# A two-layer encoder trunk on one core: the second mixer's constants get their own place and load one stage earlier, and GpSimd adds a norm's shift

## The chip, the cores and the metric

The kernel is one program on one core of a Trainium2 chip. The metric is the device time of one execution in microseconds (us); lower is better. The engines are named as in the profile: PE is TensorE (matmul), DVE is VectorE, ACT is ScalarE, POOL is GpSimd, and SP is the engine whose queue issues all the DMAs here. Each engine works through its own instructions in the order in which they stand.

## The reference, cut to what matters

The input is `x`, 256 tokens of 2048 channels in float32. Two layers follow one another; each has a mixer and a gated feed-forward, each closed by a residual sum and a layer norm with scale g and shift b:

```
for layer in range(2):
    if layer == 0: y = ab_mixer(x, ...)      # local attention and gated recurrence
    else:          y = cd_mixer(x, ...)      # pooling mixer and grouped-query attention
    x = layer_norm(DN_ALPHA * x + y, ln_mix_g[layer], ln_mix_b[layer])
    f = swiglu(x, w_gate, w_up, w_down)      # hidden width 5632
    x = layer_norm(DN_ALPHA * x + f, ln_ffn_g[layer], ln_ffn_b[layer])

def layer_norm(x, g, b):  return (x - mean) * rsqrt(var + eps) * g + b

def cd_mixer(x, ...):
    c_x, d_q, d_k, d_v = split(x @ w_in)     # 1024, 1024, 256, 256 columns
    y_c = multiscale_pool(c_x, ...)          # centred means over 2, 4, 8, 16 tokens, then a matmul
    q = rope(rms_norm(d_q, q_norm)); k = rope(rms_norm(d_k, k_norm))
    return concat(y_c, attention(q, k, d_v)) @ w_out
```

Here the place of interest is the seam between the two layers: the last norm of layer 0 (`ln_ffn_g[0]`, `ln_ffn_b[0]`) and the first projection of `cd_mixer`.

## The kernel before, in words

**Split matmuls.** Every float32 operand is split into a high part and a low part, and a product is three matmuls (`mm3`: low by high, high by high, high by low). A weight comes in halves of 128x1024 elements (512 KB). `load_half` issues the DMA into a tile `raw`, ACT casts it to `whi` (line 127), DVE subtracts to get `wlo` (line 128). There are four `raw` tiles, so a fifth load waits until the first half has been split. The `whi`/`wlo` pairs stand in a ring: four in the pool `wp`, and more in pools that a stage opens (`open_ring`); after `open_ring`, the first 12 halves still go to the four of `wp` alone. A cast waits until PE is done with the half that held its slot.

**Tokens.** The 256 tokens are two groups of 128 (`tok` 0 and 1). `mm_chunk` runs one output block of 512 columns for both groups: half by half for both groups, or, where `tok_major` is set, all halves for group 0 and then all for group 1. The outputs of a block are PSUM banks `acc`, of which there are three, so a third block's second bank is the one that the evacuation of an earlier block gives back.

**Down phase and norm.** The feed-forward has three phases, each ending in four output blocks `n` of the down projection. In the last phase `end` is true: at block `n == 1` `load_gb` loads the norm's `gam` and `bet` (1024 KB each, broadcast to all partitions), and the last block runs with `tok_major`. After each group's last matmul, `norm(tok)` takes mean and variance on DVE, the reciprocal root `rstd` on POOL (line 246, a power), centres on DVE (line 323), scales on ACT (line 337), and appends `flip(tok)` to a list. `flip` transposes the four 512-column pieces on PE (line 124, at places in the PE order that are pinned, inside the following tok_major pass), and ACT and DVE read the transposed pieces and add the shift from `betT`, which gives the next stage's operands `xTh` and `xTl`. The residual rows `res` themselves need the shift too: `flip` puts that addition into the list `idle_work`, from which a later `mm_chunk` takes two at a time and gives them to DVE, behind its weight splits (line 369).

**The mixer's constants.** `cd_mixer` opens its pool at the seam and allots the rotary tables `cc` and `sn`, the norm weights `nwq` and `nwk`, `pscale`, `rcount` and the pooling matrix `band` there. The first projection block (`kv`, tok_major) is followed by `constants_in`, which loads them; `band` passes through two of the four `raw` tiles (as `braw`) and is cast by ACT (line 875), and `nwq` is multiplied by a number on DVE (line 868). The function `kv` then evacuates the first block: ACT casts `dvh` from the bank, DVE subtracts `dvl`, ACT squares into `junk` (line 885), POOL takes `rstd`, and DVE writes `rx` from the bank (line 889), which is the last read of that bank.

**What sets the order.** The program is written through a layer whose scheduler orders each engine's instructions by priority and by its own model of time; `high_priority` raises a priority, `issue_after` and `keep_in_program_order` fix an order. Code that is moved therefore moves other instructions too.

Of the kernel before, what the change touches and what calls it, by code (L numbers as in the profile page):

```python
# [11 lines left out]
F32 = mybir.dt.float32  # L12
F32R = mybir.dt.float32r
# [5 lines left out]
P = 128  # L19
# [61 lines left out]
def trunk(ctx: ExitStack, tc: tile.TileContext, a, out):  # L81
# [216 lines left out]
    def new_stats():  # L298
        return [sm.tile([P, 4, 6], F32, tag=f"st{t}", name=f"st{t}", bufs=1) for t in range(NT)]

    def residual_tools(res, gam, bet, betT, stats):

        def evac(tok, n, psum, start, last):
            r = res[tok][:, n * NCH : (n + 1) * NCH]
            if start:
                nc.vector.scalar_tensor_tensor(r, r, ALPHA, psum, op0=mult, op1=add)
            else:
                nc.vector.tensor_tensor(r, r, psum, op=add)
            if last:
                nc.vector.bn_stats(stats[tok][:, n, :], r)  # L310

        def norm(tok, xT=None, out_rows=None):
            mv = sm.tile([P, 2], F32, tag="mv", name="mv", bufs=2)
            nc.vector.bn_aggr(mv, stats[tok])
            rstd = rstd_of(mv[:, 1:2], 1)

            def cols(j):
                s = slice(j * NCH, (j + 1) * NCH)
                return res[tok][:, s], gam[:, s], bet[:, s]

            def centre(j):
                r, g, _ = cols(j)
                return nc.vector.scalar_tensor_tensor(r, r, mv[:, 0:1], g, op0=sub, op1=mult)  # L323

            def scale(j):
                r, _, b = cols(j)
                return nc.vector.scalar_tensor_tensor(r, r, rstd[:, 0:1], b, op0=mult, op1=add)  # L327

            def store(j):
                nc.sync.dma_start(out_rows[tok * P : (tok + 1) * P, j * NCH : (j + 1) * NCH], cols(j)[0])  # L330

            if out_rows is None:
                for j in range(4):
                    dve = centre(j)
                for j in range(4):
                    r = cols(j)[0]
                    act = nc.scalar.activation(r, r, AF.Copy, scale=rstd[:, 0:1])
                ahead[:] = [dve.ins, act.ins]
                pending.append(flip(tok, xT))
            else:  # L340
                for j in (3, 0, 1):
                    tc.keep_in_program_order(centre(j))
                r, _, b = cols(3)
                nc.scalar.activation(r, r, AF.Copy, scale=rstd[:, 0:1])
                nc.gpsimd.tensor_tensor(r, r, b, op=add)
                for j in (0, 1, 2):
                    if j == 2:
                        tc.keep_in_program_order(centre(j))
                    tc.keep_in_program_order(scale(j))
                    store(j)  # L350
                store(3)

        def flip(tok, xT):
            for j in range(4):
                s = slice(j * NCH, (j + 1) * NCH)
                r = res[tok][:, s]
                with tc.high_priority(offset=1000):
                    t = mxp() if j % 2 else trp()
                    for k in range(4):
                        tc.keep_in_program_order(transpose(t[:, k * P : (k + 1) * P], r[:, k * P : (k + 1) * P], ident))  # L360
                    for part in range(2):
                        for k in range(4):
                            hi, lo = xT[0][tok][:, 4 * j + k, :], xT[1][tok][:, 4 * j + k, :]
                            tk, bk = t[:, k * P : (k + 1) * P], betT[:, 4 * j + k : 4 * j + k + 1]
                            if part == 0:
                                act = nc.scalar.activation(hi, tk, AF.Identity, bias=bk)
                            else:
                                dve = nc.vector.scalar_tensor_tensor(lo, tk, bk, hi.bitcast(F32), op0=add, op1=sub)
                idle_work.append(lambda r=r, s=s: nc.vector.tensor_tensor(r, r, bet[:, s], op=add))
                if j == 3:  # L370
                    ahead[:] = [dve.ins, act.ins]
                yield j

        return evac, norm
# [9 lines left out]


    def out_proj(w, order, groups, res, gb):
        evac, norm = residual_tools(res, *gb, new_stats())
        lhs = y_lhs(groups)
        xT = new_xT()
        for n in range(4):  # L390
            outs = [acc() for _ in range(NT)]
            halves = [(w[n, 2 * g + i], two(4 * g + 2 * i)) for g in order for i in range(2)]

            def after(tok):
                with tc.high_priority(offset=1000 if n == 3 else 0):
                    evac(tok, n, outs[tok], True, True)
                    if n == 3:
                        norm(tok, xT)

            mm_chunk(halves, lhs, outs, tok_major=(n == 3), after=after)  # L400
        return xT
# [96 lines left out]
    def ffn(layer, xT, res, mix_pool, close_mix, keep, last):  # L498
# [29 lines left out]
                if next(making[0], "end") is None:  # L528
                    later.append([3, make])

        nxt = None
        groups = {}
        for pi, chunks in enumerate(PHASES):
            end = pi == len(PHASES) - 1
# [15 lines left out]
            if end:  # L550
                stack.close()
                open_banks("uses")
                open_ring(keep(f"er{layer}"), 4)
                open_ring(later_pool(stack, f"e{layer}"), 3)
                fp = later_pool(stack, f"g{layer}")
                nxt = None if last else new_xT()
            stats = new_stats()
            evac, norm = residual_tools(res, None, None, None, stats)
            for n in range(4):
                if end and n == 1:  # L560
                    evac, norm = residual_tools(res, *load_gb(fp, layer, "ffn"), stats)
                outs = [acc() for _ in range(NT)]
                halves = [(a[f"down{layer}"][n, 2 * c + i], two(4 * ci + 2 * i)) for ci, c in enumerate(chunks) for i in range(2)]

                def after(tok):
                    with tc.high_priority(offset=1000 if end and n == 3 else 0):
                        evac(tok, n, outs[tok], pi == 0, end)
                        if end and n == 3:
                            norm(tok, nxt, out if last else None)

                mm_chunk(halves, y_lhs(gl), outs, tok_major=(end and n == 3), after=after)
# [280 lines left out]
            do[kind](i, outs)  # L852


    def cd_mixer(mp, xT, yT):
        cc = mp.tile([P, NT, P], F32, name="cc", bufs=1)
        sn = mp.tile([P, NT, P], F32, name="sn", bufs=1)
        nw = {n: mp.tile([P, P], F32, name=f"nw{n}", bufs=1) for n in ("q", "k")}
        pscale = mp.tile([P, 64], F32, name="pscale", bufs=1)[:, :8]
        rcount = mp.tile([P, 4, 2, EDGE], F32, name="rcount", bufs=1)  # L860
        band = mp.tile([P, 4, NT, T], F32R, name="band", bufs=1)

        def constants_in():
            nc.sync.dma_start(cc, a["rope_cos"])
            nc.sync.dma_start(sn, a["rope_sin"])
            for n in ("q", "k"):
                nc.sync.dma_start(nw[n], a[f"d_{n}_norm"][0:1, :].to_broadcast([P, P]))
            nc.vector.tensor_scalar(nw["q"], nw["q"], QSCALE, None, op0=mult)
            nc.sync.dma_start(pscale, a["pool_scale"])
            nc.sync.dma_start(rcount, a["rcount"])  # L870
            for g in range(0, 4, 2):
                s = slice(g, g + 2)
                raw = wp.tile([P, 2, NT, T], F32, tag="raw", name="braw", bufs=4)
                nc.sync.dma_start(raw, a["band"][:, s])
                nc.scalar.copy(band[:, s], raw)

        lhs = x_lhs(xT)
        st = {}

# [95 lines left out]
        for c, (kind, _) in enumerate(cd_plan()):  # L975
            outs = [acc() for _ in range(NT)]
            mm_chunk([(a["cd_in"][c, n], two(2 * n)) for n in range(8)], lhs, outs, tok_major=(c == 0))
            if c == 0:
                with tc.high_priority(offset=150):
                    constants_in()  # L980
            if kind == "kv":
                kv(outs)
            elif kind[0] == "q":
                q(kind[1], outs)
            else:
                pool(kind[1], outs)
# [23 lines left out]
    def layer_end(i, w, groups, yT, last):  # L1010
# [10 lines left out]
        xT = out_proj(w, groups, yT, res, load_gb(fp, i, "mix"))  # L1021
        return ffn(i, xT, res, fp, close, keep, last)

    xT = layer_end(0, a["ab_out"], AB_OUT_GROUPS, yT, False)
    yT = [new_yT() for _ in range(4)]
    with tc.tile_pool(name="cd", bufs=1, reuse_waits="tile") as mp:
        cd_mixer(mp, xT, yT)
    layer_end(1, a["cd_out"], CD_OUT_GROUPS, yT, True)
    kept.close()

# [113 lines left out]
```

## Time and profile before

| what | value |
|---|---|
| median of 3 runs | 2211.68 us (2210.59 to 2213.93) |
| profiled execution, its own time | 2208.31 us |
| its span, first to last instruction | 2206.5 us |
| mean granted TensorE clock | 0.997 of full speed |
| PE / DVE / ACT / POOL busy | 2176.5 / 1564.1 / 1053.2 / 42.2 us |
| DMA, mean | 191 GB/s, 57.0% of 16 engines |

The profiled execution lies 1.8 us above its span, and 3.4 us under the median. PE is busy nearly all the time, so a stall of PE is time of the whole; what other engines do counts where PE waits for it.

### The profile page before, as it was taken

The page shows a single profiled execution, that of the slowest core. Times are in us where ns is not written, and L with a number is a line of the kernel's source. Part 1 is how long each engine was busy: PE and PEld are TensorE (multiplying, and loading weights), DVE is VectorE, ACT ScalarE, POOL GpSimd, SP SyncE. Part 2 cuts the span into 40 slices and gives each one's busy share as a digit, 9 for nine tenths or more (in the row PEclk, how much of TensorE's full clock was granted, in tenths as well). Part 3 has the DMA queues.
Part 4 walks back from the last instruction along what each step waited for, and adds up shares of the span by engine and source line. Part 5 has one row for each costly group of instructions (what it writes and reads, how often), then busy time and mean ns, then how long its engine had stood idle before and what let it go on. Part 6 is the DMA issues. An engine that isn't in the chain of part 4 may idle for free. (4 is left out here: it accounts for less than half of the span.)

```text
span 2206.5 us, 26606 instructions
## 1 busy us (share of the span) xinstructions
PE 2176.5 (99%) x10048; PEld 1806.2 (82%) x10048; DVE 1564.1 (71%) x1960; ACT 1053.2 (48%) x1276; POOL 42.2 (2%) x43
## 2 busy tenths in 40 slices
PE   8999999999999999999999989999999999999997
PEld 7888888888888888888888778888888878888886
DVE  6886688567538787577877676677357886668865
ACT  6445544546435445445544554555344554445442
POOL 0000001000000000000000000000000000000001
PEclk9999999999999999999999999999999999999999
DMA  8555546684636565565557363657456555655573
GB/s 288 163 163 180 171 126 191 210 276 141 231 117 240 178 206 186 190 228 185 189 180 269 127 206 124 213 169 237 154 172 225 184 180 194 212 198 183 179 249 114
DMA packets 112562, 420.64 MB, mean 191 GB/s; under 512 B 13744, under 2 KB 16304, under 8 KB 105520
## 3 DMA queue, kind: packets, MB, share of 16 engines
q1 hardware_dynamic: 112432, 418.93, 57.0%
q8 instruction: 79, 1.29, 0.2%
q14 instruction: 51, 0.42, 0.1%
HBM read 416.78 MB, written 2.10 MB: 190 GB/s over the span
## 5 line engine op out<-in xcount | busy, mean ns | idle before, releaser
L128 DVE TENSOR_TENSOR wlo<-raw,whi 128x1024 fp32r<-128x1024 f32 (+1 forms) x673 | 818.8, 1224 | 435.2 <-ACT whi L127 425.0
L127 ACT CAST whi<-raw 128x1024 fp32r<-128x1024 f32 (+1 forms) x673 | 704.8, 1052 | 827.3 <-PE acc L290 329.0
L290 PE MATMUL acc<-whi,xTl 128*128 128x512 f32 x1056 | 418.3, 397 | 13.2 <-DVE rx L889 6.5
L290 PE MATMUL acc<-whi,xTh 128*128 128x512 f32 x1056 | 415.3, 393 | 0.0
L290 PE MATMUL acc<-wlo,xTh 128*128 128x512 f32 x1056 | 412.7, 393 | 1.0 <-DVE wlo L128 1.0
L290 PEld LDWEIGHTS acc<-whi,xTl 128*128 128x128 f32 x1056 | 199.8, 189 | 54.2 <-ACT whi L127 8.2
L290 PEld LDWEIGHTS acc<-wlo,xTh 128*128 128x128 f32 x1056 | 199.5, 189 | 42.6 <-DVE wlo L128 1.9
L290 PEld LDWEIGHTS acc<-whi,xTh 128*128 128x128 f32 x1056 | 199.8, 189 | 39.2
L290 PE MATMUL acc<-whi,yTl 128*128 128x512 f32 x512 | 200.4, 392 | 0.1
L290 PE MATMUL acc<-whi,yTh 128*128 128x512 f32 x512 | 199.5, 390 | 0.0
L290 PE MATMUL acc<-wlo,yTh 128*128 128x512 f32 x512 | 197.7, 390 | 0.0
L290 PE MATMUL aside<-whi,xTl 128*128 128x512 f32 x336 | 131.2, 390 | 0.4 <-ACT g L480 0.4
L290 PE MATMUL bside<-whi,xTl 128*128 128x512 f32 x336 | 131.2, 390 | 0.1
L290 PE MATMUL bside<-whi,xTh 128*128 128x512 f32 x336 | 131.0, 390 | 0.0
L290 PE MATMUL aside<-whi,xTh 128*128 128x512 f32 x336 | 131.0, 390 | 0.0
L290 PE MATMUL bside<-wlo,xTh 128*128 128x512 f32 x336 | 128.2, 390 | 0.0
L290 PE MATMUL aside<-wlo,xTh 128*128 128x512 f32 x336 | 128.1, 390 | 0.0
L290 PEld LDWEIGHTS acc<-wlo,yTh 128*128 128x128 f32 x512 | 96.1, 188 | 20.4 <-DVE wlo L128 0.5
L290 PEld LDWEIGHTS acc<-whi,yTl 128*128 128x128 f32 x512 | 96.1, 188 | 19.9 <-DVE yTl L973 0.3
L290 PEld LDWEIGHTS acc<-whi,yTh 128*128 128x128 f32 x512 | 96.2, 188 | 19.3
L128 DVE TENSOR_TENSOR sl<-z,sh 128x2048 fp32r<-128x2048 f32 x44 | 100.7, 2289 | 6.2 <-ACT sh L127 5.6
L439 ACT CAST sh<-rs 128x1536 fp32r<-128x1536 f32 x44 | 65.2, 1483 | 74.7 <-DMA rs<-in_gu 32.9
(257 smaller groups left out, 3109.5 us busy)
## 6 DMA issues: line engine op xcount, KB each, us to landing
raw<-in_gu SPq DMA_DIRECT2D x264, 512.0 KB, 4.7
raw<-in_down SPq DMA_DIRECT2D x176, 512.0 KB, 3.6
raw<-in_ab_in SPq DMA_DIRECT2D x127, 512.0 KB, 4.1
rs<-in_gu SPq DMA_DIRECT2D x44, 1024.0 KB, 5.8
raw<-in_cd_in SPq DMA_DIRECT2D x40, 512.0 KB, 4.1
raw<-in_ab_out SPq DMA_DIRECT2D x32, 512.0 KB, 4.4
raw<-in_cd_out SPq DMA_DIRECT2D x32, 512.0 KB, 4.4
x<-in_xT SPq DMA_DIRECT2D x8, 256.0 KB, 6.4
```

Of the source, the lines that this page charges most:

```text
L127: nc.scalar.copy(hi, src)
L128: return nc.vector.tensor_tensor(lo, src, hi.bitcast(F32), op=sub).ins
L290: ins = nc.tensor.matmul(o, lhs[a], rhs[b], start=start and n == 0, stop=stop and n == 2)
L439: nc.scalar.copy(hi[:, :3], raw[:, :3])
```

## The change

`cd_constants` is a new function with the body of `constants_in`; it is called in the last down phase of layer 0, at block `n == 1` and ahead of `load_gb`, and takes its tiles from a pool `cdc` that is opened ahead of the ring `er0` and kept open through the mixer. `residual_tools` gets an argument `defer`: `out_proj` passes True and so keeps the list `idle_work`; the feed-forward's norm (only layer 0's has a `flip`) now gives the eight additions of `bet` to POOL, right where `flip` is done with a piece.

```diff
-    def residual_tools(res, gam, bet, betT, stats):
+    def residual_tools(res, gam, bet, betT, stats, defer=False):
...
-                idle_work.append(lambda r=r, s=s: nc.vector.tensor_tensor(r, r, bet[:, s], op=add))
+                if defer:
+                    idle_work.append(lambda r=r, s=s: nc.vector.tensor_tensor(r, r, bet[:, s], op=add))
+                else:
+                    nc.gpsimd.tensor_tensor(r, r, bet[:, s], op=add)
...
     def out_proj(w, order, groups, res, gb):
-        evac, norm = residual_tools(res, *gb, new_stats())
+        evac, norm = residual_tools(res, *gb, new_stats(), True)
...
             if end:
                 stack.close()
                 open_banks("uses")
+                cdp = None if last else keep("cdc")
                 open_ring(keep(f"er{layer}"), 4)
...
             for n in range(4):
+                if cdp and n == 1:
+                    consts.extend(cd_constants(cdp))
                 if end and n == 1:
                     evac, norm = residual_tools(res, *load_gb(fp, layer, "ffn"), stats)
...
+    def cd_constants(pool):
+        cc = pool.tile([P, NT, P], F32, name="cc", bufs=1)
+        sn = pool.tile([P, NT, P], F32, name="sn", bufs=1)
+        nc.sync.dma_start(cc, a["rope_cos"])
+        nc.sync.dma_start(sn, a["rope_sin"])
+        nw = {}
+        for n in ("q", "k"):
+            nw[n] = pool.tile([P, P], F32, name=f"nw{n}", bufs=1)
+            nc.sync.dma_start(nw[n], a[f"d_{n}_norm"][0:1, :].to_broadcast([P, P]))
+        nc.vector.tensor_scalar(nw["q"], nw["q"], QSCALE, None, op0=mult)
...
+        band = pool.tile([P, 4, NT, T], F32R, name="band", bufs=1)
+        for g in range(0, 4, 2):
+            s = slice(g, g + 2)
+            raw = wp.tile([P, 2, NT, T], F32, tag="raw", name="braw", bufs=4)
+            nc.sync.dma_start(raw, a["band"][:, s])
+            nc.scalar.copy(band[:, s], raw)
+        return cc, sn, nw, pscale, rcount, band
...
-            if c == 0:
-                with tc.high_priority(offset=150):
-                    constants_in()
```

How the instructions stand. First SP's queue from the last down phase on, before (`in_down` are the weights of the down projection, `in_cd_in` those of the second mixer's first projection, `braw` is `band` on its way):

```order
L168 DMA raw<-in_down 128x1024 x10
L379 DMA gam<-in_ln_ffn_g 128x2048
L380 DMA bet<-in_ln_ffn_b 128x2048
L382 DMA betT<-in_ln_ffn_bT 128x16
L168 DMA raw<-in_down 128x1024 x22
L168 DMA raw<-in_cd_in 128x1024 x8
L874 DMA braw<-in_band 128x1024 x2
L168 DMA raw<-in_cd_in 128x1024 x10
L864 DMA cc<-in_rope_cos 128x256
L865 DMA sn<-in_rope_sin 128x256
L867 DMA nwq<-in_d_q_norm 128x128
L867 DMA nwk<-in_d_k_norm 128x128
```

The same place of SP's queue, changed:

```order
L168 DMA raw<-in_down 128x1024 x8
L879 DMA braw<-in_band 128x1024 x2
L864 DMA cc<-in_rope_cos 128x256
L865 DMA sn<-in_rope_sin 128x256
L869 DMA nwq<-in_d_q_norm 128x128
L869 DMA nwk<-in_d_k_norm 128x128
L168 DMA raw<-in_down 128x1024 x3
L872 DMA pscale<-in_pool_scale 128x8
L874 DMA rcount<-in_rcount 128x64
L382 DMA gam<-in_ln_ffn_g 128x2048
L383 DMA bet<-in_ln_ffn_b 128x2048
L168 DMA raw<-in_down 128x1024
```

The tables `cc` to `nwk` stood behind 50 weight loads of these two stages (10, 22, 8 and 10), `braw` behind 40; all now stand behind the first 8 of the down phase. `gam` and `bet` moved from behind the 10th load to behind the 11th, with the constants ahead of them.

DVE from the transposes of group 1 on, before (`xTl` is the norm's result, `wlo` a weight split, `dvl` and `rx` belong to `kv`):

```order
L368 SCALAR_TENSOR_TENSOR xTl_9132<-mx,betT,xTh_9130 128x128 x4
L128 TENSOR_TENSOR wlo<-raw,whi 128x1024 x5
L369 TENSOR_TENSOR res_3796<-res_3796,bet 128x512 x2
L128 TENSOR_TENSOR wlo<-raw,whi 128x1024
L369 TENSOR_TENSOR res_3796<-res_3796,bet 128x512 x2
L128 TENSOR_TENSOR wlo<-raw,whi 128x1024
L369 TENSOR_TENSOR res_3797<-res_3797,bet 128x512 x2
L128 TENSOR_TENSOR wlo<-raw,whi 128x1024
L369 TENSOR_TENSOR res_3797<-res_3797,bet 128x512 x2
L868 TENSOR_SCALAR nwq<-nwq 128x128
L128 TENSOR_TENSOR dvl<-acc,dvh 128x256 x2
```

The same place on DVE, changed:

```order
L368 SCALAR_TENSOR_TENSOR xTl_9135<-mx,betT,xTh_9133 128x128 x4
L128 TENSOR_TENSOR wlo<-raw,whi 128x1024 x2
L128 TENSOR_TENSOR dvl<-acc,dvh 128x256
L128 TENSOR_TENSOR wlo<-raw,whi 128x1024 x2
L245 TENSOR_SCALAR rstd<-ss 128x2
L128 TENSOR_TENSOR wlo<-raw,whi 128x1024
L897 SCALAR_TENSOR_TENSOR rx<-acc,rstd,nwk 128x128 x2
L128 TENSOR_TENSOR wlo<-raw,whi 128x1024
L903 TENSOR_TENSOR ry<-rx,sn 128x128 x2
L128 TENSOR_TENSOR wlo<-raw,whi 128x1024
L128 TENSOR_TENSOR dvl<-acc,dvh 128x256
```

The first `dvl` stood behind all eight weight splits of the next block and the eight shifts, and now stands behind two splits; the first `rx` stands behind five. The multiplication of `nwq` has gone forward into the down phase, behind the last `yTl` of the feed-forward; ACT's two casts of `band` stand at the same place there, behind the last `yTh`.

POOL at the same seam (`rstd` is the power of a norm; the rows of one piece of the difference, - before and + changed):

```order
-L818 TENSOR_TENSOR bias<-bias,colmask 128x512 x2
-L246 TENSOR_TENSOR rstd<-rstd,mhalf 128x1 x4
+L824 TENSOR_TENSOR bias<-bias,colmask 128x512 x2
+L246 TENSOR_TENSOR rstd<-rstd,mhalf 128x1 x3
+L372 TENSOR_TENSOR res_3796<-res_3796,bet 128x512 x4
+L246 TENSOR_TENSOR rstd<-rstd,mhalf 128x1
+L372 TENSOR_TENSOR res_3797<-res_3797,bet 128x512 x4
 L246 TENSOR_TENSOR rstd<-rstd,mhalf 128x2 x2
 L246 TENSOR_TENSOR rstd<-rstd,mhalf 128x4 x4
```

The power of group 1's norm, which stood right behind that of group 0, now stands behind four additions for group 0.

More of the change, by code (lines that the diff above doesn't have):

```diff
@@ L529, in make @@
                     later.append([3, make])
-        nxt = None
+        nxt = cdp = None
         groups = {}
@@ L852, in ab_mixer @@
             do[kind](i, outs)
[L855 to L875, printed above, removed]
+    def cd_constants(pool):
[8 more added lines that the diff above has]
+        nc.vector.tensor_scalar(nw["q"], nw["q"], QSCALE, None, op0=mult)
+        pscale = pool.tile([P, 64], F32, name="pscale", bufs=1)[:, :8]
+        nc.sync.dma_start(pscale, a["pool_scale"])
+        rcount = pool.tile([P, 4, 2, EDGE], F32, name="rcount", bufs=1)
+        nc.sync.dma_start(rcount, a["rcount"])
+        band = pool.tile([P, 4, NT, T], F32R, name="band", bufs=1)
[5 more added lines that the diff above has]
+        return cc, sn, nw, pscale, rcount, band
@@ L877, in cd_mixer @@
+    def cd_mixer(mp, consts, xT, yT):
+        cc, sn, nw, pscale, rcount, band = consts
         lhs = x_lhs(xT)
@@ L1022, in layer_end @@
         return ffn(i, xT, res, fp, close, keep, last)
+    consts = []
     xT = layer_end(0, a["ab_out"], AB_OUT_GROUPS, yT, False)
@@ L1026, in trunk @@
     with tc.tile_pool(name="cd", bufs=1, reuse_waits="tile") as mp:
-        cd_mixer(mp, xT, yT)
+        cd_mixer(mp, consts, xT, yT)
     layer_end(1, a["cd_out"], CD_OUT_GROUPS, yT, True)
```

## The prediction

> **What bounds the kernel now.** I read the page first. Its first part gives each engine's busy time, share of the span and instructions:
>
> ```profile
> PE 2176.5 (99%) x10048; PEld 1806.2 (82%) x10048; DVE 1564.1 (71%) x1960; ACT 1053.2 (48%) x1276; POOL 42.2 (2%) x43
> ```
>
> PE is the bound everywhere; a change gains only what PE loses: gaps, and time at a lower clock. So next the busy time by stretch of the seam (length, then each engine's busy time and count, granted clock, DMA share, GB/s), and the waits of PE there (total, times, longest):
>
> ```profile
> 1233.70:1256.00 22.30, 22.30 (x108) 18.48 (x107) 15.51 (x37) 12.55 (x29) 0.99 (x1) 1.00 0.34 115
> 1256.00:1270.00 14.00, 12.54 (x53) 9.12 (x52) 9.91 (x12) 6.41 (x7) 0.00 (x0) 1.00 0.59 187
> 1270.00:1285.00 15.00, 8.49 (x27) 6.47 (x28) 8.51 (x22) 7.04 (x22) 2.57 (x3) 0.77 0.61 204
> PE acc L290 <- DVE rx L889: 6.5, 1, 6.5
> ```
>
> The tok_major pass (first row) has no gap. The next block loses 1.5 us, then 6.5 us in one wait, and the clock is 0.77 around it. The timeline of PE shows it matmul by matmul:
>
> ```profile
> 1258.11 0.39 PE L290 MATMUL acc<-whi,xTl 128*128 128x512 f32 x1
> ...
> 1265.37 0.39 PE L290 MATMUL acc<-wlo,xTh 128*128 128x512 f32 x1
> ...
> 1270.68 0.39 PE L290 MATMUL acc<-wlo,xTh 128*128 128x512 f32 x1
> 1277.58 0.76 PE L290 MATMUL acc<-whi,xTl 128*128 128x512 f32 x1 [6.51 <-DVE rx L889]
> ...
> 1282.40 0.39 PE L290 MATMUL acc<-wlo,xTh 128*128 128x512 f32 x1
> ```
>
> The undisturbed pace is 32 matmuls from 1258.11 to 1265.37: 0.227 us each. From 1265.37 to 1270.68 there are 12 steps in 5.31 us, 2.59 too many: weight splits come late. From 1270.68 to 1277.58 one step takes 6.90, 6.67 too many. From 1277.58 to 1282.40 stand 11 steps in 4.82, 2.32 too many: half pace after the gap. Together **11.6 us**.
>
> Why the bank is late, by the timelines of SP, ACT and DVE:
>
> ```profile
> 1229.45 1.46 SPq L874 DMA_DIRECT2D braw<-in_band  x2
> 1232.76 37.42 SPq L168 DMA_DIRECT2D raw<-in_cd_in  x10
> 1270.23 0.42 SPq L864 DMA_DIRECT2D cc<-in_rope_cos  x1
> 1268.47 1.98 ACT L875 CAST band<-braw 128x1024 fp32r<-128x1024 f32 x2
> 1270.36 0.64 ACT L127 CAST dvh<-acc 128x256 fp32r<-128x256 f32 x2
> 1274.44 0.23 DVE L868 TENSOR_SCALAR nwq<-nwq 128x128 f32<-128x128 f32 x1 [3.41 <-DMA nwq<-in_d_q_norm]
> 1276.82 0.61 DVE L889 SCALAR_TENSOR_TENSOR rx<-acc,rstd,nwk 128x128 f32<-128x128 f32 x2
> ```
>
> `braw` is issued at 1229 but cast only at 1268, behind ACT's weight casts; until then two of the four `raw` tiles are lost, and ten loads need 37 us of SP's queue. The tables stand behind them. DVE waits for `nwq`, and the evacuation of a block that PE ended near 1257 starts at 1270 on ACT and frees its bank at 1277.
>
> **The change, part by part.**
>
> *Constants early.* Eight transfers (the two `braw`, `cc`, `sn`, `nwq`, `nwk`, `pscale`, `rcount`) leave the seam, and with them the 11.6 us: the `raw` tiles are four again (no 2.59), and the evacuation follows the projection instead of a DMA. What is late next? By the changed order the first `rx` stands behind five `wlo` of the next block, and the fifth load can be issued when the first half is split:
>
> ```profile
> 1248.96 2.60 DVE L128 TENSOR_TENSOR wlo<-raw,whi 128x1024 fp32r<-128x1024 f32 x2
> raw<-in_cd_in SPq DMA_DIRECT2D x40, 512.0 KB, 4.1
> bet<-in_ln_ffn_b SPq DMA_DIRECT2D x2, 1024.0 KB, 8.4
> 1163.87 1.05 ACT L127 CAST whi<-raw 128x1024 fp32r<-128x1024 f32 x1 [1.67 <-PE acc L290]
> ```
>
> The first split ends near 1250.3, the load lands at 1254.4 by its 4.1 us, ACT's cast (1.05) and DVE's split (half of 2.60) make it 1256.7, and two `rx` (0.61) 1257.4; the small steps between (`junk`, `rstd`) run beside that load. PE's tok_major pass ends 48 matmuls (10.9 us) and the 2.6 us of late splits before the big gap opens at 1270.9, so at 1257.4, and the changed order puts 15 matmuls, 3.4 us, ahead of the first that needs the bank: 1260.8. That leaves 3.4 us. I take no wait there; with the longest landing in this stretch of the program, 8.4 us instead of 4.1, PE would wait 0.9 us. Less than nothing it can't be, since PE then runs without a gap.
>
> *The same transfers in the down phase.* They go past the 9th to 32nd down load on SP, and `gam` and `bet` go behind them. ACT's weight casts there are released by PE (the row above), so weights wait for PE, not PE for weights:
>
> ```profile
> 1152.06 0.42 SPq L379 DMA_DIRECT2D gam<-in_ln_ffn_g  x1
> 1154.74 0.68 DVE L128 TENSOR_TENSOR yTl<-tr,yTh 128x512 fp32r<-128x512 f32 x1
> nwq<-in_d_q_norm SPq DMA_DIRECT2D x1, 64.0 KB, 3.2
> braw<-in_band SPq DMA_DIRECT2D x2, 512.0 KB, 5.8
> 1160.00:1195.00 35.00, 35.00 (x156) 28.96 (x156) 25.44 (x26) 18.58 (x18) 0.00 (x0) 1.00 0.79 270
> ```
>
> A half lasts 12 matmuls, 2.72 us, and four are ready ahead: a cast may come 3 halves, 8.2 us, after its slot is free, less 2.4 us of cast and split, so some 5.8 us late before PE waits. ACT's two casts of `band` cost 1.98 us; the second `braw` takes the place of the 10th load, just ahead of 1152.06, lands by 5.8 us near 1157.5, and the eighth half's cast behind it starts near 1158.5 where it started near 1155.7 (three halves before the 1163.87): 2.8 us late, inside the 5.8. DVE meets `nwq` at 1155.4 (end of the `yTl` row); it is issued three places behind 1152, near 1153.0, and lands 3.2 to 8.4 us later, 1156.2 to 1161.4. I take 1157.5, since 3.2 is the row of `nwq` itself and only `braw` is ahead; at 1161.4 the eighth split would still end at 1162.9, before PE ends the seventh half at 1163.87. The tightest is the 12th load: the 10th is issued when the eighth split ends, near 1160, then come the 11th, two tables, `gam` and `bet`, and the 12th near 1162.5. With 8.4 us it lands at 1170.9, is split at 1173.3, and PE comes to it four halves after 1163.87 (the end of the seventh), at 1174.7: spare 1.4 us. Two loads more in the queue (1.9 us each at the 270 GB/s of this phase) would make it 2.4 us late. I take zero, and keep 0 to 2.4 us for the range; a gain is excluded, as PE has no gap here. The megabyte of `band` and the tables cost some 5 us of transfer in all, against a ring of eleven halves, 30 us.
>
> *The shift on POOL.* Eight additions leave DVE and become POOL's. The price of one, and what two engines do to each other:
>
> ```profile
> 351.61 7.19 POOL L818 TENSOR_TENSOR bias<-bias,colmask 128x512 f32<-128x512 f32 x1 [3.31 <-DMA bias<-in_na_bias]
> 396.24 1.30 POOL L818 TENSOR_TENSOR bias<-bias,colmask 128x512 f32<-128x512 f32 x1 [2.69 <-DMA bias<-in_na_bias]
> 396.40 2.22 DVE L128 TENSOR_TENSOR wlo<-raw,whi 128x1024 fp32r<-128x1024 f32 x1 [1.53 <-ACT whi L127]
> 1261.28 1.29 DVE L369 TENSOR_TENSOR res<-res,bet 128x512 f32<-128x512 f32 x2
> ```
>
> On DVE a pair took 1.29 us, so 5.2 us go from it, on which no wait of PE rests once the constants are early. On POOL one takes 1.3 us; begun while DVE runs one instruction with two SBUF inputs after another, it lasted 7.19; and a `wlo` (half of 2.36 us alone) that meets a running addition is held to 2.22. [...] What decides is POOL's own order, since group 1's `rstd` stands behind group 0's four additions:
>
> ```profile
> 1227.83 0.60 PE L124 MATMUL tr<-ident,res 128*128 128x128 f32 x4
> 1228.20 2.36 DVE L128 TENSOR_TENSOR wlo<-raw,whi 128x1024 fp32r<-128x1024 f32 x2 [0.16 <-ACT whi L127]
> 1231.52 1.22 DVE L128 TENSOR_TENSOR wlo<-raw,whi 128x1024 fp32r<-128x1024 f32 x1
> 1237.30 2.73 DVE L323 SCALAR_TENSOR_TENSOR res<-res,mv,gam 128x512 f32<-128x512 f32 x4
> 1237.46 0.99 POOL L246 TENSOR_TENSOR rstd<-rstd,mhalf 128x1 f32<-128x1 f32 x1 [13.28 <-DVE rstd L243]
> 1238.49 2.56 ACT L337 ACTIVATE res<-res,rstd 128x512 f32<-128x512 f32 x4 [3.40 <-POOL rstd L246]
> 1240.59 0.60 PE L124 MATMUL tr<-ident,res 128*128 128x128 f32 x4
> ```
>
> The first addition may start at 1228.4, `rstd` was wanted at 1237.46: 9.0 us for four. DVE's weight splits hold the first two back to about 1230.5 and 1233 (the two `wlo` rows; the second starts 0.3 later behind the addition); from there DVE reads PSUM mostly, so the four end near 1237, on time. ACT's first piece ends about 1239.2, PE transposes it at 1240.59, so a delay of 1.4 us is still free. I take zero; the upper end of the likely case is one addition held through DVE's four centring instructions (2.73) plus its own 1.3, less 1.4: 2.6 us.
>
> *Sum.* 2.59 + 6.67 + 2.32 = 11.6 saved, less 0.3 for a `wlo` held up here or there: 11.3 us. On the profiled execution the span goes from 2206.5 to 2195.2, its own time from 2208.3 to 2197.0; on the median of the runs, 3.4 us higher, 2211.7 to **2200.4**.
>
> **The rivals.**
>
> *A. As summed, 66%:* 2198 to 2203; the low end is a gain of 13, if DVE's relief also takes out small gaps later in the mixer.
>
> *B. A part is given back, 17%:* the held addition (2.6 us), the 12th down load (2.4 us) or the late bank (0.9 us): 2203 to 2206. For it speaks the 7.19; against it that DVE has only three such splits in those 9 us.
>
> *C. The bank stays late, 10%:* the evacuation of `kv` now stands between in-order casts, and if loads are slower than their 4.1 us, each link adds. Half of the 11.6 would stay, or all: 2206 to 2212, about 2208. That the change then does nothing is its far end: the tables come early, but PE's wait only changes its releaser.
>
> *D. Slower, 7%:* POOL starves. If each of the four additions lasts 7.19, `rstd` is issued at 1228.4 + 28.8 = 1257.2, 19.7 late; PE stands 18.3 at the pinned transposes, plus 2.3 at half clock, less 11.6 saved: 9.0 slower, 2220.7. It decides from 4.9 us an addition on (19.7 for four: the 9.0 there are, 1.4 of slack, 11.6 less 2.3). Against it: the 7.19 arose where DVE had hardly another kind of instruction; here only the three splits are of it, until the centring.
>
> **How the numbers follow.** Likeliest is A, 2200.4. The range leaves out D and most of C: 2197.8 to 2206.5. About 0.2%, 4.4 us, is what a measurement can tell from no change; A, B and a quarter of C are faster by more (0.85), most of C is the same (0.08), D slower (0.07).
>
> **What would show it.** Right: no wait of PE over 1 us between the tok_major pass and the second block's end, granted clock 1.00 there; `dvl` on DVE near 1252, `rx` before 1260; POOL's additions 1.3 to 2 us each, `rstd` of group 1 within 1.4 us of its old distance from the transposes; no PE wait in the down phase. Wrong: a PE wait ahead of a transpose of `res`, released by ACT and behind it POOL (B, D); one at `acc` released by `rx` (C); one at the 12th down half released by a load (B).

## The result, and the profile after

| | before | changed |
|---|---|---|
| median of 4 runs each | 2212.36 us (2210.59 to 2213.93) | 2199.43 us (2197.47 to 2205.05) |
| ratio | | 0.9950, 95% interval 0.9938 to 0.9962 |
| profiled execution, its span | 2206.5 us | 2197.7 us |

By the medians the changed kernel is 12.9 us faster; by the ratio, which is not the quotient of the two medians, it is 11.1 us (8.4 to 13.7 by the interval). A gain of 11.3 us and a median of 2200.4 were predicted. The span of the profiled execution fell by 8.8 us, to 2197.7 where 2195.2 was predicted. First the page's busy times after:

```profile
PE 2172.2 (99%) x10048; PEld 1804.3 (82%) x10048; DVE 1560.4 (71%) x1952; ACT 1052.4 (48%) x1276; POOL 50.9 (2%) x51
```

DVE has eight instructions fewer, POOL eight more. Then the seam by stretch, in the columns and at the times shown of before:

```profile
1233.70:1256.00 22.30, 22.01 (x107) 17.98 (x106) 19.70 (x45) 15.04 (x35) 10.07 (x8) 1.00 0.42 139
1256.00:1270.00 14.00, 14.00 (x65) 11.55 (x64) 11.59 (x21) 7.93 (x12) 0.70 (x1) 1.00 0.80 273
1270.00:1285.00 15.00, 15.00 (x69) 12.39 (x68) 8.76 (x15) 7.75 (x22) 1.65 (x2) 1.00 0.69 214
```

In the second and third row PE was busy 12.54 of 14.00 and 8.49 of 15.00 us before, in the third at a clock of 0.77; now it has no gap there, at 1.00. A small gap stands in the first row, which had none.

To measure the place without the rest of the program, I take one stretch of PE: from the first transpose of the norm at the seam to the first of the next norm. In each kernel here it holds the same 1108 PE instructions. Its ends by the timeline of PE, before (the first end stands in the prediction, 1227.83) and changed:

```profile
1469.32 0.60 PE L124 MATMUL tr<-ident,res 128*128 128x128 f32 x4
```

```profile
1228.03 0.60 PE L124 MATMUL tr<-ident,res 128*128 128x128 f32 x4
1459.23 0.60 PE L124 MATMUL tr<-ident,res 128*128 128x128 f32 x4
```

That is 241.49 us before and 231.21 after (231.20 by the rounded rows): 10.3 us. The waits of PE within the stretch (total, times, longest), before and changed:

```profile
PE acc L290 <- DVE rx L889: 6.5, 1, 6.5
PE acc L290 <- DVE wlo L128: 1.0, 2, 0.5
PE mx L290 <- DVE ptl L128: 0.5, 1, 0.5
PE acc L290 <- ACT whi L127: 0.3, 1, 0.3
```

```profile
PE mx L290 <- DVE ptl L128: 1.2, 1, 1.2
PE acc L290 <- DVE wlo L128: 0.3, 1, 0.3
```

The long wait and the late splits are gone, and a wait at `ptl` (attention of the mixer) has grown. Outside the stretch both programs wait here and there; the end of the program, from the stretch on, took 737.21 us before and 738.47 after, and 735.6 to 744.1 in the other kernels below. This scatter is the reason why a stretch tells apart what a median of runs cannot. A stretch is one execution all the same: two profiles of the changed kernel, below, differ by 0.5 us.

### The profile page after: what moved, and what is told of

Its sections match the earlier page's. It is cut to its first block, busy times and chain, and to the rows that moved or that the text cites. A ratio compares the mean times of both kernels' runs of the same rounds, so it can differ in the third digit from the quotient of the medians.

```text
span 2197.7 us, 26611 instructions
## 1 busy us (share of the span) xinstructions
PE 2172.2 (99%) x10048; PEld 1804.3 (82%) x10048; DVE 1560.4 (71%) x1952; ACT 1052.4 (48%) x1276; POOL 50.9 (2%) x51
## 3 DMA queue, kind: packets, MB, share of 16 engines
q8 instruction: 79, 1.29, 0.2%
```

## The experiments

Theory 1, that of the prediction: the late constants cost the 11.6 us, the additions as such are worth nothing. The rival: the additions on DVE are what counts. The kernels with one part alone and the two with one kind of constants late were run first and together; theory 2, below, was formed from them. All ratios are to the kernel before on the same chip.

**The constants alone.** Undone: the additions.

```diff
-                    evac, norm = residual_tools(res, *load_gb(fp, layer, "ffn"), stats)
+                    evac, norm = residual_tools(res, *load_gb(fp, layer, "ffn"), stats, True)
```

> The constants early, the eight additions back in the list that DVE takes from. Theory 1 (the prediction: the 11.6 us came from the late constants, the additions as such are worth nothing): 2199 to 2202 us, no wait of PE over 1 us at the second block; DVE's order puts the first rx behind all eight weight splits and the additions again, near 1268, and PE, whose order puts 48 matmuls ahead of the bank there (1257.4 + 10.9 = 1268.3), just meets it. Rival (the additions were needed, since with them on DVE the evacuation stays last in its order): PE waits for the bank 2 to 6 us and works some us at half clock after it: 2203 to 2209 us.

Measured: 2200.06 beside 2210.18 us, ratio 0.9952 (0.9940 to 0.9964). The stretch is 229.85 us, 11.64 under before; 11.6 was predicted. DVE's timeline, and all that PE waits for in the stretch:

```profile
1263.94 1.28 DVE L370 TENSOR_TENSOR res<-res,bet 128x512 f32<-128x512 f32 x2
1267.38 0.61 DVE L897 SCALAR_TENSOR_TENSOR rx<-acc,rstd,nwk 128x128 f32<-128x128 f32 x2
```

```profile
PE mx L290 <- DVE ptl L128: 0.5, 1, 0.5
```

The additions are done on DVE at 1265.2, the bank is given back at 1268.0, and PE comes to it at 1269.4 without a wait. The evacuation still stands last in DVE's order here, with 1.4 us to spare. The theory holds: the constants alone are worth all of it.

**The additions alone.** The kernel before, with the additions on POOL:

```diff
+                if defer:
...
+                else:
+                    nc.gpsimd.tensor_tensor(r, r, bet[:, s], op=add)
```

> The eight additions on POOL, the constants loaded late as before. Theory 1 (the late constants are the loss): DVE waits for nwq ahead of the first evacuation and two raw tiles are held by braw, so most of the 11.6 us stays: 2207 to 2213 us. Rival (the additions alone free the order: with them gone, the evacuation and the loads of nwq stand far forward, and the late constants then cost little): 2200 to 2205 us.

Measured: 2201.16 beside 2210.18 us, ratio 0.9959 (0.9947 to 0.9971); the stretch is 230.91 us, 10.58 under before. Here the theory missed and the rival hit: the additions alone also bring it. ACT and DVE, by their timelines:

```profile
1253.55 1.99 ACT L878 CAST band<-braw 128x1024 fp32r<-128x1024 f32 x2
1254.82 0.22 DVE L871 TENSOR_SCALAR nwq<-nwq 128x128 f32<-128x128 f32 x1
1263.00 0.60 DVE L892 SCALAR_TENSOR_TENSOR rx<-acc,rstd,nwk 128x128 f32<-128x128 f32 x2
```

`band` is cast at 1253.55, behind two weight casts of the block, where it was 1268.47 behind eight; `nwq` is there without a wait, where DVE waited 3.41 us; the bank comes free at 1263.6 instead of 1277.4. The constants still stand in the mixer, but everything that they hold up has moved forward. Theory 2: what counts in the additions is not the DVE time that POOL takes over but the order that comes with the list (which ties its additions behind weight splits).

**The additions at once, but on DVE.** As the last one, with the other engine:

```diff
-                    nc.gpsimd.tensor_tensor(r, r, bet[:, s], op=add)
+                    nc.vector.tensor_tensor(r, r, bet[:, s], op=add)
```

> Constants late as before; the eight additions stay on DVE, but are given at once where flip is done with a piece, not through the list. Theory 2 (the list, tied to the last weight split, keeps the evacuation behind all splits; what the additions do for the time is the order that they leave): the evacuation stands forward as with POOL, and the time is 8 to 10 us under before, with up to 1 us lost at group 1's transposes, since three additions (0.65 us each) now stand ahead of its centring on DVE against 1.4 us of slack. Rival (DVE's time is what POOL relieves: 5.2 us): the gain is gone or halved, 0 to 5 us under before.

Measured: 2199.72 beside 2210.23 us, ratio 0.9964 (0.9951 to 0.9977); stretch 232.31 us, 9.18 under before. DVE has all its work, the constants are late, and nearly all of the gain is there: it is the order. Whether the tie behind the splits makes that order, or only the later place in the program, was not tested apart. POOL's relief is worth 1.4 us (232.31 against 230.91), of which 1.1 stands ahead of group 1's transposes, as expected:

```profile
1241.46 0.66 PE L124 MATMUL tr<-ident,res 128*128 128x128 f32 x4 [1.05 <-ACT res L337]
```

**Which of the constants.** Four kernels: `band` late alone or the tables late alone, each with the additions on POOL and in DVE's list. The late ones have their tiles in the mixer's pool and their loads behind the `kv` block again, as before:

```diff
-        cc, sn, nw, pscale, rcount, band = consts
+        cc, sn, nw, pscale, rcount = consts
+        band = mp.tile([P, 4, NT, T], F32R, name="band", bufs=1)
...
+            if c == 0:
+                with tc.high_priority(offset=150):
+                    constants_in()
```

> As changed, but band alone is loaded late again, through two raw tiles; the tables stay early. Theory 1 (the late splits of the second block come from the two held raw tiles, the long wait from the tables): the 2.6 us of late splits are back, the wait for the bank is not: 2201 to 2204 us. Rival (the held tiles also delay the evacuation): 2205 to 2210 us. If band's casts stand early enough on ACT that the tiles are free in time: 2199 to 2201.

> As changed, but the tables (cc, sn, nwq, nwk, pscale, rcount) are loaded late again; band stays early. Theory 1 (a wait of DVE for nwq ahead of the evacuation holds the bank): nwq stands third on DVE behind two splits and is issued behind 12 loads, so DVE waits 2 to 5 us there, the spare 3.4 us of the bank is used up, and PE waits 0 to 3 us: 2199 to 2205 us. Rival (the tables do nothing, band's tiles are all): 2199 to 2201, no wait of DVE over 1 us for nwq.

Measured: `band` late 2201.22, ratio 0.9959 (0.9947 to 0.9971); the tables late 2198.97, ratio 0.9952 (0.9940 to 0.9964), beside 2210.18 us. The stretches are 231.00 and 230.91 us: with the additions on POOL neither costs anything. The expected 2.6 us of late splits did not come back, since ACT frees the tiles early, and DVE does not wait for `nwq`, which was expected late; the last of the three cases of the first and the rival of the second are right:

```profile
1252.87 2.00 ACT L885 CAST band<-braw 128x1024 fp32r<-128x1024 f32 x2
```

```profile
1253.17 0.22 DVE L883 TENSOR_SCALAR nwq<-nwq 128x128 f32<-128x128 f32 x1
```

The same with the additions in DVE's list:

> Additions in DVE's list as before, tables early, band alone late through two raw tiles. In this order ACT casts band behind all eight weights of the second block, so the tiles are held as before. Theory 1 (the prediction's pieces: late splits by the held tiles 2.6 us, the rest by casts of band and the wait for nwq): the 2.6 us stay; the evacuation starts at 1271 instead of 1274.7, as DVE's 3.4 us for nwq are gone, and PE waits about 3.2 us instead of 6.7, then 0 to 2.3 us of half clock: 3.5 to 5.8 us less than before. Rival (the tables were the whole long wait): 9 us less than before.

> Additions in DVE's list as before, band early, the tables alone late. Theory 1 (in this order the evacuation comes last anyway, near 1267, and with four raw tiles SP's queue gets to nwq near 1265.4): nwq lands 3.2 to 5 us later, DVE meets it 0 to 3 us late, PE waits 0 to 2 us: 9.5 to 11.6 us less than before. Rival (the tables were the long wait): the 6.7 us stay, only the 2.6 us of late splits and the half clock can go: 2.6 to 5 us less than before.

Measured, beside 2210.23 us: `band` late 2205.12, ratio 0.9984 (0.9970 to 0.9999), stretch 237.89, 3.60 under before; the tables late 2198.98, ratio 0.9955 (0.9943 to 0.9967), stretch 231.73, 9.76 under before. Both as theory 1 had it. The profile with `band` late is of its slowest run, 2220.13 us; what made that run long lies outside the stretch (8.5 us more than before ahead of it, 6.9 behind it). With `band` late, ACT casts it behind the eight weights, PE waits, and then runs at half clock (the third row is a stretch, as above, PEclk third from the end):

```profile
1276.89 1.99 ACT L885 CAST band<-braw 128x1024 fp32r<-128x1024 f32 x2
1282.36 0.77 PE L290 MATMUL acc<-whi,xTl 128*128 128x512 f32 x1 [2.87 <-DVE rx L899]
1284.00:1286.00 2.00, 2.00 (x6) 1.52 (x6) 1.75 (x6) 1.04 (x1) 1.18 (x1) 0.50 0.93 372
```

With the tables late, what is left of the long wait, at full clock:

```profile
1267.25 0.23 DVE L883 TENSOR_SCALAR nwq<-nwq 128x128 f32<-128x128 f32 x1 [2.90 <-DMA nwq<-in_d_q_norm]
1268.26 0.47 PE L290 MATMUL acc<-whi,xTl 128*128 128x512 f32 x1 [1.56 <-DVE rx L899]
1268.00:1270.00 2.00, 1.74 (x8) 1.47 (x9) 1.93 (x9) 0.68 (x3) 0.00 (x0) 1.00 0.26 85
```

All in one table, the stretch in us:

| constants | additions in DVE's list | on POOL at once |
|---|---|---|
| all late | 241.49 (before) | 230.91 |
| `band` late | 237.89 | 231.00 |
| tables late | 231.73 | 230.91 |
| all early | 229.85 | 231.21 (changed) |

The loss needs both: the list that keeps the evacuation back, and the late constants, `band` for most of it (8.0 of the 11.6, by 237.89 less 229.85; the tables alone cost 1.9). Either remedy removes it, and the second one then adds nothing. The values from 230.7 to 231.2 can't be told apart, by the 0.5 us between two profiles of one kernel.

**Rival D, made to happen.** Group 0's additions done twice on POOL:

```diff
-                    nc.gpsimd.tensor_tensor(r, r, bet[:, s], op=add)
+                    for _ in range(2 if tok == 0 else 1):
+                        nc.gpsimd.tensor_tensor(r, r, bet[:, s], op=add)
```

> As changed, with each of group 0's four additions on POOL done twice (the shift of group 0's rows is so added twice). Rival D of the prediction, made on purpose: the eight stand ahead of group 1's rstd. They took 2.03, 2.27, 2.27 and 1.29 us; eight at 1.3 to 2.3 us from 1228.8 on end at 1241 to 1245, so rstd starts 2.5 to 6.5 us later than in the changed kernel, whose slack of 1.4 us is used up already: PE stands 2.5 to 6.5 us ahead of group 1's transposes, plus 0 to 2.3 us of half clock: 2202 to 2208, 2.5 to 8.8 us over the changed kernel. If rstd's delay is hidden elsewhere: as the changed kernel, within 1 us.

Measured: 2205.36 beside 2210.23 us, ratio 0.9977 (0.9967 to 0.9987). The stretch is 235.59, 4.4 over the changed kernel. The timelines of POOL, DVE and PE:

```profile
1231.15 13.60 POOL L373 TENSOR_TENSOR res<-res,bet 128x512 f32<-128x512 f32 x8 [4.37 <-PE tr L124]
1241.05 4.91 DVE L323 SCALAR_TENSOR_TENSOR res<-res,mv,gam 128x512 f32<-128x512 f32 x4
1244.71 0.99 POOL L246 TENSOR_TENSOR rstd<-rstd,mhalf 128x1 f32<-128x1 f32 x1
1246.51 0.66 PE L124 MATMUL tr<-ident,res 128*128 128x128 f32 x4 [3.17 <-ACT res L337]
1247.00:1249.00 2.00, 2.00 (x8) 1.55 (x7) 0.00 (x0) 2.00 (x4) 1.28 (x1) 0.55 0.00 0
```

Eight additions (1.70 us each) push `rstd` back, PE waits 3.2 us at the transposes behind it, and runs at about half clock after that (0.55 in the last row). The road of rival D, a late `rstd`, exists; with four additions it was just not taken. What rival D gave as its reason, additions of 7.19 us each, did not come even here.

**The spare of the down phase.** The changed kernel, with `band` loaded and cast twice there:

```diff
-        for g in range(0, 4, 2):
+        for g in (0, 2, 0, 2):
```

> As changed, but band is loaded and cast twice in the down phase: two more transfers of 512 KB and two more casts there. Theory 1 (the constants are hidden in the down phase by a spare of only about 1 us at its tightest load): gam and bet now stand ahead of the 10th load, which lands near 1173.5 and is split near 1176, where PE wants it at 1169.5; the 9th is some 1.4 us late behind the second pair of casts. PE waits 5 to 7 us in the down phase, plus 0 to 2.3 us at half clock: 5 to 9 us over the changed kernel. Rival (the ring of eleven halves, 30 us, covers it): no wait, the changed kernel's time.

Measured: 2205.69 beside 2210.10 us, ratio 0.9969 (0.9957 to 0.9981). There is a wait where there was none, though a smaller one than expected:

```profile
1173.00 1.04 ACT L127 CAST whi<-raw 128x1024 fp32r<-128x1024 f32 x1 [5.10 <-DMA raw<-in_down]
1174.10 0.50 PE L290 MATMUL acc<-whi,yTl 128*128 128x512 f32 x1 [1.76 <-ACT whi L127]
1174.00:1176.00 2.00, 1.86 (x7) 1.23 (x8) 1.23 (x1) 0.64 (x2) 0.00 (x0) 1.00 0.85 346
```

By the trace the down phase is 2.4 us longer (from the 141st `whi`,`yTh` matmul of the program to the first transpose: 77.00 us, 74.60 in the changed kernel and in before); the clock stays 1.00. The 9th half was in time after all, and of the 10th I had put the landing 3 us too late. Of the 5.7 us by which its median lies over the changed kernel's beside it, 2.4 are so explained; the rest is within what the runs scatter and stays open.

**The changed kernel and the constants alone, on one chip.**

> The changed kernel once more, beside the constants alone on the same chip: 2198 to 2201 us, and from the first transpose of the norm at the seam to the first of the next norm 231.2 us, as in its first profile.

> The constants early, the additions in DVE's list, once more, beside the changed kernel. Theory 2 (the additions on POOL bring nothing once the constants are early, and cost what DVE's splits lose beside them and what the other order costs later): 1.4 us under the changed kernel from the first transpose of the norm at the seam to that of the next (229.8 against 231.2), which the median of the runs can hardly tell: 0 to 3 us faster. Rival (they are worth a little of their own): the changed kernel is faster by 0 to 2 us.

Measured, beside 2210.10 us: changed 2199.95 (2195.65 to 2205.99), ratio 0.9947 (0.9931 to 0.9963); constants alone 2200.78 (2196.38 to 2201.59), ratio 0.9947 (0.9934 to 0.9960). By the runs they can't be told apart. The stretches are 230.70 and 229.85 us: the constants alone are 0.9 us shorter, 1.4 in the first pair, with the same 229.85 twice. So the additions on POOL cost about a microsecond of PE here; no version was found that is measurably faster than the changed kernel.

## Why the prediction was right

*The sum.* 11.3 us were predicted, 12.9 and 10.2 measured on two chips (2212.36 to 2199.43, 2210.10 to 2199.95), and 10.3 and 10.8 in the stretch. The three terms (2.59, 6.67, 2.32) are right as a sum: the constants alone gave 11.64. That the median came within 1.0 us of 2200.4 is partly luck: the four runs of the changed kernel spread over 7.6 us, and the profiled span missed by 2.5 us, half of which (1.3 us) lies behind the stretch.

*The evacuation.* "`dvl` on DVE near 1252, `rx` before 1260", the two `rx` done at 1257.4:

```profile
1252.22 0.42 DVE L128 TENSOR_TENSOR dvl<-acc,dvh 128x256 fp32r<-128x256 f32 x1
1256.73 0.60 DVE L897 SCALAR_TENSOR_TENSOR rx<-acc,rstd,nwk 128x128 f32<-128x128 f32 x2
```

They were done at 1257.33.

*The down phase.* DVE was to wait for `nwq` until 1157.5, the 12th load to leave a spare of 1.4 us. The 12th is the single `in_down` of SP's queue; its cast and split follow:

```profile
1157.85 0.23 DVE L870 TENSOR_SCALAR nwq<-nwq 128x128 f32<-128x128 f32 x1 [2.23 <-DMA nwq<-in_d_q_norm]
1160.61 0.39 SPq L168 DMA_DIRECT2D raw<-in_down  x1
1171.59 1.05 ACT L127 CAST whi<-raw 128x1024 fp32r<-128x1024 f32 x1 [6.46 <-DMA raw<-in_down]
1172.67 4.87 DVE L128 TENSOR_TENSOR wlo<-raw,whi 128x1024 fp32r<-128x1024 f32 x4 [3.77 <-ACT whi L127]
1160.00:1195.00 35.00, 35.00 (x156) 28.98 (x155) 24.18 (x25) 18.18 (x18) 0.00 (x0) 1.00 0.89 316
```

It was split by 1173.9, and PE came to it at 1174.9 (1163.87, later by the 0.2 of this run, and four halves): spare 1.0 us. PE was busy 35.00 of 35.00 us. The load itself took 10.9 us, longer than the 8.4 that I had taken for the worst case; it was issued earlier than I thought, and the two errors nearly cancel. Two more transfers there and PE waits, as the experiment showed. So the 30 us of cover that the prediction counts for a ring of eleven halves are not there for these loads: the first 12 halves go to four slots alone.

*The additions on POOL: the term that was too small.* Of POOL's own time the working was right (four that end near 1237, ended at 1236.5). But I took 0.3 us off the gain for them, and it was 1.36 in the first pair (231.21 less 229.85) and 0.85 in the second. The timelines of POOL, DVE and PE in the first profile show where:

```profile
1228.76 7.75 POOL L372 TENSOR_TENSOR res<-res,bet 128x512 f32<-128x512 f32 x4 [4.37 <-PE tr L124]
1228.41 3.46 DVE L128 TENSOR_TENSOR wlo<-raw,whi 128x1024 fp32r<-128x1024 f32 x2 [0.17 <-ACT whi L127]
1238.83 0.99 POOL L246 TENSOR_TENSOR rstd<-rstd,mhalf 128x1 f32<-128x1 f32 x1 [2.32 <-DVE rstd L243]
1243.37 1.29 POOL L372 TENSOR_TENSOR res<-res,bet 128x512 f32<-128x512 f32 x1 [0.55 <-ACT whi L127]
1243.38 2.36 DVE L128 TENSOR_TENSOR wlo<-raw,whi 128x1024 fp32r<-128x1024 f32 x1 [1.99 <-ACT whi L127]
1245.11 0.40 PE L290 MATMUL acc<-whi,xTh 128*128 128x512 f32 x1
1245.80 0.50 PE L290 MATMUL acc<-wlo,xTh 128*128 128x512 f32 x1 [0.29 <-DVE wlo L128]
```

The first additions hold two splits up by 1.1 us (3.46 for 2.36), so DVE comes late to group 1's statistics. `rstd` starts at 1238.83 for 1237.46, which is 1.17 us later by the distance from the first transpose: inside the 1.4 us of slack that the prediction gave it. `rstd` waits for DVE, not for POOL's additions. The next held split (2.36 for 1.22) is the one that PE needs: 0.69 us from one matmul to the next where 0.23 is its pace, so 0.5 us lost. In the second profile of the changed kernel the same split begins 0.02 us ahead of the addition (1245.34 on POOL), is not held, and PE loses nothing there:

```profile
1245.32 1.23 DVE L128 TENSOR_TENSOR wlo<-raw,whi 128x1024 fp32r<-128x1024 f32 x1 [1.98 <-ACT whi L127]
```

So held splits cost 0.5 us or nothing, around the 0.3 us taken. What the sum lacked is the wait at `ptl`, DVE and PE there in the changed kernel, then before:

```profile
1380.02 0.68 DVE L966 COPY ppt<-mx 128x512 f32<-128x512 f32 x1
1380.62 0.68 DVE L128 TENSOR_TENSOR ptl<-tr,pth 128x512 fp32r<-128x512 f32 x1
1381.36 0.38 PE L290 MATMUL mx<-ptl,dvh 128*128 128x256 f32 x1 [1.25 <-DVE ptl L128]
```

```profile
1390.33 0.69 DVE L128 TENSOR_TENSOR ptl<-tr,pth 128x512 fp32r<-128x512 f32 x1
1390.93 0.68 DVE L958 COPY ppt<-mx 128x512 f32<-128x512 f32 x1
1391.07 0.39 PE L290 MATMUL mx<-ptl,dvh 128*128 128x256 f32 x1 [0.49 <-DVE ptl L128]
```

The copy has moved ahead of the split that PE waits for, 0.76 us. This wait is 1.2 to 1.3 us in every kernel here whose additions are not in DVE's list, and 0.5 in every other: another order, not another speed.

*The rivals.* A came true. Of B only the held splits came, with 0.5 us or nothing and not the 2.6 of its worst case; C did not (no wait at `acc` for `rx`), and D's late `rstd` needs about twice the additions.

*What the prediction did not see.* It said of the 5.2 us that go from DVE that no wait rests on them "once the constants are early", which the first experiment confirms. It did not ask the opposite: whether the constants matter once the additions are gone. They do not (230.91). Nor did it see that "the evacuation follows the projection" is the work of the other part. With the constants alone the first `rx` are done at 1268.0, not before 1260, and the spare is 1.4 us, not 3.4. The number came out right because either part is enough; credited to the constants alone, it is right only in the order that the list gave.

*The move to POOL.* Once the constants are early, the move of the additions from DVE's list to POOL cost 0.9 to 1.4 us of the stretch. With the constants late, POOL was 1.4 us better than the same additions given at once on DVE (230.91 against 232.31).

## What to carry to other kernels

Where two parts of a change could each remove the same wait, run each alone: their gains need not add up, and here either was the whole. Look at what an instruction's place in an engine's order keeps behind it before you count its own time; eight additions of 0.65 us cost nothing by themselves, and with the constants late what they kept back cost 11 us. A load that is moved under a phase with full cover still needs its tightest neighbour worked out; here one microsecond was left.

## What the runs showed of the hardware

An addition on POOL and a weight split on DVE met in both profiles of the changed kernel. In the first the addition begins 0.01 us first, at 1243.37, and takes 1.29 us, as the one at 1241.53 does while DVE stands idle; the split takes 2.36 instead of 1.22. In the second the split begins 0.02 us first, at 1245.32, and takes its 1.23; the addition takes 2.36 instead of 1.29. In the kernel with doubled additions DVE's centring, which met them, took 4.91 us; in the changed kernel, where it met none, it took 2.73.

PE's granted clock was 0.50 behind waits of 2.87 us (`band` late, additions in DVE's list) and 6.51 us (before), 0.55 in the stretch of 2 us behind one of 3.17 us (doubled additions), and 1.00 behind waits of 1.56 us (tables late, additions in DVE's list) and 1.76 us (`band` twice). But the length of a wait alone does not tell these apart. With `band` late and the additions in DVE's list the clock was 0.50 behind a wait of 1.85 us, earlier in the program; with the additions alone it stayed 1.00 behind one of 2.03 (eight transposes in 1.25 us, as in before at a clock of 1.00, and not in 1.53):

```profile
566.52 1.53 PE L124 MATMUL tr<-ident,sil 128*128 128x128 f32 x8 [1.85 <-DVE sil L519]
567.35:570.76 3.41, 3.41 (x11) 2.81 (x10) 2.06 (x3) 1.57 (x3) 0.00 (x0) 0.50 0.78 253
1519.62 1.25 PE L124 MATMUL tr<-ident,sil 128*128 128x128 f32 x8 [2.03 <-DVE sil L519]
```

So one wait near 2 us went with 3.41 us at half clock and the other with none; what made the difference was not shown.

With `band` late, the clock was 0.50 from 1280.7 to 1287.6; from the end of the wait 12 matmuls ran in 5.24 us where 2.72 is the pace, which is another 2.5 us. That wait of 2.87 us cost nearly twice its length.
